# Feed-forward inputs without the norm: differences made from them, gate and up scaled afterwards, pairs from the third block on

## The chip, the cores and the metric

One Trainium2 chip; the kernel runs on one of its cores. A core has TensorE (matmuls, into PSUM), VectorE (DVE in the profile), ScalarE (ACT), GpSimd (POOL) and SyncE (SP), which issues most of the DMA transfers. Each engine takes its instructions in a fixed order and waits by semaphores. The metric is the device time of one execution in microseconds; lower is better.

## The reference

Two layers; each is a half-step feed-forward, a mixer (attention and a state-space part) and a second half-step feed-forward, on 512 positions of 1024 channels, float32.

```
h = rms_norm(x, gain)                    # x * rs(position) * gain(channel)
gate, up = split(h @ w_up)               # 2 x 2816 columns
x = x + 0.5 * ((silu(gate) * up) @ w_down)
```

`rs` is one number per position, so (x * gain) @ w, multiplied by rs afterwards, is h @ w.

## The kernel before, in words

Activations lie with channels on partitions, as eight tiles of 128x512 (`KB` = 8). A float32 product is made of three matmuls (`mm3`, L284 to L286): each operand is split into a rounded part "hi" and a rest "lo", and hi*hi, lo*hi and hi*lo are summed. A weight *unit* is 128x1024: SyncE loads it (`wraw`), ScalarE makes `whi` (L251), VectorE makes `wlo` (L253). `whi` and `wlo` have three buffers, and `convert` is set going two units ahead.

`h` holds the eight (hi, lo) tiles that the matmuls stream. When x is finished, `norm_split` writes them as x * gain, without rs, since rs needs the sum of squares over all channels (`norm_square`, `norm_end`: a matmul with ones, then the root). So a stage starts on unnormalised `h`. Once rs is there, `scale_blocks` (L334) makes normalised tiles `tt`, and at the next "up" `project` swaps: `swapped` (L325, L326) splits `tt` into new tiles, which later units use.

**The feed-forward** (`ffn`) takes 22 blocks of 128 hidden channels in three slices (8, 8, 6); after each slice "down" products add to x. A plain block is two units, gate and up, each 24 matmuls of 512 columns (8 channel tiles x 3). Blocks from `pairs_from` on are taken two at a time by `pair_of_blocks` with seven products of half size in place of eight: inputs and weights are cut into quarters (lower and upper channels; first and second half of the positions; gate and up), and the products, in the order "11", "12", "s2", "s1", "s3", "s4", "22", take quarters or their sums and differences. Each is 24 matmuls of 256 columns. Two use the accumulator `chain` again, so what it holds is copied out by ScalarE between products (`g1`, `g2`, L578, L583). The differences of inputs are made once in a feed-forward by `combine` (L346 to L357; results `th` and `tt`), from normalised tiles, after the swap.

Sums of weights come in two ways. s1 and s3 are made by DMA: SyncE loads a stored block, and GpSimd issues a second transfer that adds another to it (L225). s2 and s4 are added by VectorE (`add`, L236). In a pair g1 and g2 go through `activate` (L565 Silu on ScalarE, L570 product with up on VectorE, then a split).

**What sets the order.** TensorE, VectorE, ScalarE and GpSimd run in the order in which the program writes their instructions. `spawn` adds a generator to a list, and `tick` advances all of them once; a tick comes after each k of a plain product and after every second k in a pair, and `yield n` rests for n ticks. SyncE's issues are ordered by the scheduler.

Of the kernel before, what the change touches and what calls it, by code (L numbers as in the profile page):

```python
# [16 lines left out]
P = 128  # L17
# [70 lines left out]
def pairs_from(layer, f):  # L88

    return 6 if (layer, f) == (0, 1) else 4  # L90
# [49 lines left out]
class Builder:  # L140
# [6 lines left out]
    SPARE = 2  # L147

    def __init__(self, ctx, tc, xT, wflat, par, taps, out):
# [62 lines left out]
    def fetch(self, i):  # L212
# [8 lines left out]
        for key in self.early.get(i, ()):  # L221
            base = key[:-1]
            raw = self.sums[key] = self.t(self.sx, [P, KB * P], key[-1], bufs=2)
            self.nc.sync.dma_start(raw, self.stored(base + ("s1",)))
            self.nc.gpsimd.dma_start(raw, self.stored(base + ("22" if key[-1] == "s1" else "11",)), accum_op=ALU.add)  # L225
# [75 lines left out]
    def project(self, *key, swap=False, aside=False):  # L301
# [5 lines left out]
        if swap and not normed and self.scaled_blocks >= KB // 2:  # L307
# [6 lines left out]
            if self.th is not None:  # L314
                self.spawn(self.combine())
# [23 lines left out]
    def combine(self):  # L339
# [3 lines left out]
        a, b = slice(0, half), slice(half, SEQ)  # L343
        for k in range(KB // 2):
            u, v = self.tt[k], self.tt[k + KB // 2]
            nc.vector.tensor_tensor(u[:, a], u[:, a], u[:, b], op=ALU.subtract)  # L346
# [4 lines left out]
            for i in (k, k + KB // 2):  # L351
                yield 1
                hi = self.th[i]
                nc.scalar.copy(hi, self.tt[i])
                yield 2
                lo = self.t(self.tp, [P, SEQ], "tt", F32R)
                nc.vector.tensor_tensor(lo, self.tt[i], hi.bitcast(F32), op=ALU.subtract)  # L357
                self.diff[i] = (hi, lo)
# [159 lines left out]
    def gate(self, pg, g, normed):  # L518
        nc = self.nc
        if normed:  # L520
            self.tables(False)
            nc.scalar.activation(g, pg, AF.Silu)
        else:
            yield from self.scaled(g, pg)
            yield 3
            self.tables(False)
            nc.scalar.activation(g, g, AF.Silu)
            yield 1
            nc.gpsimd.tensor_tensor(g, g, self.rs, op=ALU.mult)
        self.gated[g.name] = True  # L530
        yield 1
# [9 lines left out]
    def pair_of_blocks(self, base, fp, two):  # L541
# [4 lines left out]
        assert self.normed and self.combined == n  # L546
# [16 lines left out]
        def activate(g, c, cols):  # L563

            nc.scalar.activation(g, g, AF.Silu)  # L565
            yield 1
            while not c:
                yield 1
# [5 lines left out]

        up1, up2 = [], []
# [745 lines left out]
```

## Time and profile before

| | |
|---|---|
| median of 3 runs | 2631.35 us (2630.26 to 2632.52) |
| the profiled execution's own time | 2631.69 us |
| its span, first to last instruction | 2630.0 us |
| TensorE granted clock, mean | 0.997 |
| busy: PE / DVE / ACT / POOL | 99% / 64% / 49% / 15% of the span |
| pairs of blocks | 35 (70 accumulating DMAs of GpSimd) |

Times in rows are microseconds from the span's start. A row of the timeline is: start, length, engine, line, operation, output<-inputs, shapes, count, and in brackets how long the engine was idle before it and what ended that. Successive instructions overlap a little, so their spacing is read from their starts.

### The profile page before, as it was taken

Reading aid. Unit: us, or ns where it says so; the run is one execution under the profiler, and the core shown is the slowest. Engines: PE = TensorE matmul, PEld = TensorE weight load, DVE = VectorE, ACT = ScalarE, POOL = GpSimd, SP = SyncE. Lnnn points to the kernel's source line nnn. Section 1 sums busy time; section 2 is a strip of 40 time slices with the busy share of each in tenths; the row PEclk is TensorE's granted clock in tenths of the full one; section 3 lists DMA queues with packets and bytes.
Section 4 is the critical chain, followed back from the end, with each engine's and each line's share of the span. In section 5 each row is a group of like instructions: output and inputs, shape, how many; then the busy total and the mean of one; then the engine's idle time right before and its main releaser. Section 6 shows DMA issues by size and latency. Waiting matters only on the chain.

```text
span 2630.0 us, 37423 instructions
## 1 busy us (share of the span) xinstructions
PE 2601.0 (99%) x14784; PEld 2282.8 (87%) x14784; DVE 1680.4 (64%) x2322; ACT 1277.5 (49%) x2069; POOL 385.5 (15%) x542
## 2 busy tenths in 40 slices
PE   9999999999999999999999999999999999999998
PEld 6899988888888889899988989888888888899996
DVE  8565675665666468575785746766666754775655
ACT  5343546655554245353553535566555643443444
POOL 2000011133232011000110000112332410200001
PEclk9999999999999999999999999999999999999999
DMA  6555342333333446474354644423333344464632
GB/s 187 143 148 149 105 137 75 97 112 105 109 96 119 142 136 163 120 191 112 124 143 135 169 129 114 128 75 110 102 116 105 97 136 122 134 170 131 175 110 74
DMA packets 101551, 331.59 MB, mean 126 GB/s; under 512 B 11856, under 2 KB 13136, under 8 KB 101376
## 3 DMA queue, kind: packets, MB, share of 16 engines
q1 hardware_dynamic: 91008, 292.43, 35.5%
q0 software_dynamic: 10080, 36.70, 8.1%
q8 instruction: 116, 1.90, 0.3%
q14 instruction: 59, 0.48, 0.1%
q10 hardware_dynamic: 288, 0.07, 0.0%
HBM read 316.48 MB, written 12.68 MB: 125 GB/s over the span
## 4 chain that ended last, share of the span: by engine, by line
PE 86%; DVE 9%; ACT 2%; issue 1%; DMA 1%; POOL 0%; SPq 0%; DVEq 0%; ACTq 0%
PE mm L284 24%; PE mm L286 24%; PE mm L285 24%; PE pa L285 3%; PE pa L286 3%; DVE wlo L253 3%; PE pa L284 3%; PE pa L975 1%; PE pt L738 1%; DVE tt L334 1%; PE pa L812 1%; PE pa L977 1%; DVE hlo L468 1%; PE pt L960 1%; PE pt L958 1%
## 5 line engine op out<-in xcount | busy, mean ns | idle before, releaser
L251 ACT CAST whi<-wraw 128x1024 fp32r<-128x1024 f32 (+2 forms) x437 | 436.7, 999 | 532.6 <-PE mm L286 507.7
L253 DVE TENSOR_TENSOR wlo<-wraw,whi 128x1024 fp32r<-128x1024 f32 (+2 forms) x437 | 541.7, 1240 | 187.8 <-ACT whi L251 185.9
L284 PE MATMUL mm<-hhi,whi 128*128 128x512 f32 (+1 forms) x1728 | 650.3, 376 | 0.0
L286 PE MATMUL mm<-hlo,whi 128*128 128x512 f32 (+1 forms) x1728 | 631.4, 365 | 1.9 <-DVE hlo L326 1.8
L285 PE MATMUL mm<-hhi,wlo 128*128 128x512 f32 (+1 forms) x1728 | 629.3, 364 | 0.7 <-DVE wlo L253 0.6
L286 PEld LDWEIGHTS mm<-hlo,whi 128*128 128x128 f32 x1728 | 326.3, 189 | 57.6 <-DVE hlo L326 3.7
L285 PEld LDWEIGHTS mm<-hhi,wlo 128*128 128x128 f32 x1728 | 327.2, 189 | 47.1 <-DVE wlo L253 1.5
L284 PEld LDWEIGHTS mm<-hhi,whi 128*128 128x128 f32 x1728 | 326.9, 189 | 44.8 <-issue 1.0
L284 PE MATMUL mm<-act,whi 128*128 128x512 f32 x704 | 274.0, 389 | 0.0
L285 PE MATMUL mm<-act,wlo 128*128 128x512 f32 x704 | 274.0, 389 | 0.0
L286 PE MATMUL mm<-act,whi 128*128 128x512 f32 x704 | 273.9, 389 | 0.0
L285 PE MATMUL mm<-th,wlo 128*128 128x256 f32 x840 | 238.0, 283 | 1.7 <-DVE wlo L253 1.7
L286 PE MATMUL mm<-tt,whi 128*128 128x256 f32 x840 | 237.7, 283 | 0.0
L284 PE MATMUL mm<-th,whi 128*128 128x256 f32 x840 | 237.7, 283 | 0.0
L253 DVE TENSOR_TENSOR wlo<-s,whi 128x1024 fp32r<-128x1024 f32 x140 | 171.2, 1224 | 69.2 <-ACT whi L251 68.0
L598 DVE SCALAR_TENSOR_TENSOR x<-mm,x 128x512 f32<-128x512 f32 x96 | 66.1, 688 | 209.0 <-PE mm L286 209.0
L225 POOL DMA_DIRECT2D s<-in_wflat_dram x70 | 60.9, 938 | 915.9 <-DMA s<-in_wflat_dram 417.4
L251 ACT CAST whi<-s 128x1024 fp32r<-128x1024 f32 x140 | 146.4, 1046 | 39.4 <-PE mm L286 39.3
L285 PEld LDWEIGHTS mm<-th,wlo 128*128 128x128 f32 x840 | 161.2, 192 | 2.3 <-DVE wlo L253 2.3
L284 PEld LDWEIGHTS mm<-th,whi 128*128 128x128 f32 x840 | 161.3, 192 | 0.0
L286 PEld LDWEIGHTS mm<-tt,whi 128*128 128x128 f32 x840 | 161.3, 192 | 0.0
L876 DVE SCALAR_TENSOR_TENSOR cv<-mm,conv,cv 128x511 f32<-128x511 f32 (+2 forms) x192 | 142.4, 743 | 24.2 <-ACT cv L873 22.3
(264 smaller groups left out, 4653.4 us busy)
## 6 DMA issues: line engine op xcount, KB each, us to landing
wraw<-in_wflat_dram SPq DMA_DIRECT2D x357, 512.0 KB, 3.7
s<-in_wflat_dram SPq DMA_DIRECT2D x70, 512.0 KB, 5.4
s<-in_wflat_dram POOLq DMA_DIRECT2D x70, 512.0 KB, 7.6
wraw<-in_wflat_dram SPq DMA_DIRECT2D x64, 384.0 KB, 3.0
cumb<-cum_d SPq DMA_DIRECT2D x16, 768.0 KB, 4.2
xd<-x SPq DMA_DIRECT2D x16, 256.0 KB, 4.2
wraw<-in_wflat_dram SPq DMA_DIRECT2D x16, 256.0 KB, 3.2
x<-xd SPq DMA_DIRECT2D x16, 256.0 KB, 5.0
```

Source lines behind the costliest of these rows:

```text
L225: self.nc.gpsimd.dma_start(raw, self.stored(base + ("22" if key[-1] == "s1" else "11",)), accum_op=ALU.add)
L251: nc.scalar.copy(hi[:, :n], raw[:, :n])
L253: nc.vector.tensor_tensor(lo[:, :n], raw[:, :n], hi[:, :n].bitcast(F32), op=ALU.subtract)
L284: mm(ps, a[0], b[0], start=start, stop=False, **kw)
L285: mm(ps, a[1], b[0], start=False, stop=False, **kw)
L286: mm(ps, a[0], b[1], start=False, stop=stop, **kw)
L334: self.nc.vector.scalar_tensor_tensor(self.tt[k], self.x[k], gain[:, k:k + 1], self.rs, op0=ALU.mult, op1=ALU.mult)
L468: nc.vector.scalar_tensor_tensor(lo, x, gain[:, m:m + 1], hi.bitcast(F32), op0=ALU.mult, op1=ALU.subtract)
L598: self.nc.vector.scalar_tensor_tensor(x, pd, 0.5, x, op0=ALU.mult, op1=ALU.add)
L738: self.nc.tensor.transpose(pt[:, cs], src[:, cs], self.ident)
L812: nc.tensor.matmul(pz[:, (i - j) * P:n], lhs, part, start=False, stop=(i == j and part is sps[i][1]), skip_group_check=True)
L876: nc.vector.scalar_tensor_tensor(u[:, i:], ps[:, :SEQ - i], tap[KCONV - 1 - i], u[:, i:], op0=ALU.mult, op1=ALU.add)
```

## The change

- `pairs_from` goes from 4 to 2, and from 6 to 4 in the first feed-forward: one more pair in each of the four.
- In a feed-forward `h` stays x * gain. There is no `scale_blocks`, no swap and no second set of tiles.
- `combine` starts as soon as x is finished (in the first feed-forward 10 ticks after the opening) and makes the differences from x * gain itself, with two ScalarE activations added for each two tiles.
- A plain gate is multiplied by rs on VectorE ahead of Silu and on GpSimd behind it, which scales the product with up as well; before, this was so only for blocks ahead of the swap.
- In a pair, g1 is multiplied by rs on GpSimd ahead of Silu and again behind it; g2 is on VectorE, and the up that goes with it (c) on GpSimd (`normed_up`).
- GpSimd's accumulating transfer for s1 and s3 is issued 9 ticks behind the load (`onto`) instead of at once, and not ahead of the feed-forward's own fifth unit (`first`).
- `norm_end` waits 6 ticks instead of 4 ahead of its matmul.

```diff
 def pairs_from(layer, f):
-    return 6 if (layer, f) == (0, 1) else 4
+    return 4 if (layer, f) == (0, 1) else 2
...
+            if key[2:] == ("gate", 0):
+                first = i + 4
             if "pair" in key and key[-1] in ("s1", "s3"):
-                self.early.setdefault(i - (5 if key[-1] == "s1" else 4), []).append(key)
+                self.early.setdefault(max(first, i - (5 if key[-1] == "s1" else 4)), []).append(key)
...
         for key in self.early.get(i, ()):
-            base = key[:-1]
-            raw = self.sums[key] = self.t(self.sx, [P, KB * P], key[-1], bufs=2)
-            self.nc.sync.dma_start(raw, self.stored(base + ("s1",)))
-            self.nc.gpsimd.dma_start(raw, self.stored(base + ("22" if key[-1] == "s1" else "11",)), accum_op=ALU.add)
+            raw = self.t(self.sx, [P, KB * P], key[-1], bufs=2)
+            self.nc.sync.dma_start(raw, self.stored(key[:-1] + ("s1",)))
+            self.spawn(self.onto(key, raw), 9)
+
+    def onto(self, key, raw):
+        src = self.stored(key[:-1] + ("22" if key[-1] == "s1" else "11",))
+        self.nc.gpsimd.dma_start(raw, src, accum_op=ALU.add)
+        self.sums[key] = raw
+        yield 1
...
-    def combine(self):
+    def combine(self, gain):
...
+        while len(self.h) < KB:
+            yield 1
         for k in range(KB // 2):
-            u, v = self.tt[k], self.tt[k + KB // 2]
-            nc.vector.tensor_tensor(u[:, a], u[:, a], u[:, b], op=ALU.subtract)
+            m = k + KB // 2
+            u, v, x = self.tt[k], self.tt[m], self.x[k]
+            nc.scalar.activation(u[:, b], x[:, b], AF.Copy, scale=gain[:, k:k + 1])
+            nc.scalar.activation(v, self.x[m], AF.Copy, scale=gain[:, m:m + 1])
+            yield 1
+            nc.vector.scalar_tensor_tensor(u[:, a], x[:, a], gain[:, k:k + 1], u[:, b], op0=ALU.mult, op1=ALU.subtract)
             nc.vector.tensor_tensor(u[:, b], v[:, b], u[:, b], op=ALU.subtract)
...
-    def gate(self, pg, g, normed):
+    def gate(self, pg, g):
         nc = self.nc
-        if normed:
-            self.tables(False)
-            nc.scalar.activation(g, pg, AF.Silu)
-        else:
-            yield from self.scaled(g, pg)
-            yield 3
-            self.tables(False)
-            nc.scalar.activation(g, g, AF.Silu)
-            yield 1
-            nc.gpsimd.tensor_tensor(g, g, self.rs, op=ALU.mult)
+        yield from self.scaled(g, pg)
+        yield 3
+        self.tables(False)
+        nc.scalar.activation(g, g, AF.Silu)
+        yield 1
+        nc.gpsimd.tensor_tensor(g, g, self.rs, op=ALU.mult)
...
         def activate(g, c, cols):
+            while self.rs is None:
+                yield 1
+            norm(nc.gpsimd if c is up1 else nc.vector, g, cols)
+            yield 2 if c is up1 else 1
+            self.tables(False)
             nc.scalar.activation(g, g, AF.Silu)
             yield 1
+            if c is up1:
+                norm(nc.gpsimd, g, cols)
+                yield 1
             while not c:
                 yield 1
...
+        def normed_up(c):
+            while self.rs is None:
+                yield 1
+            norm(nc.gpsimd, c, b)
+            up2.append(c)
+
+        def norm(eng, r, cols):
+            r = r.rearrange("p (j t) -> p j t", j=2)
+            eng.tensor_tensor(r, r, self.rs[:, cols].unsqueeze(1).to_broadcast([P, 2, half]), op=ALU.mult)
...
-            yield from self.norm_end(3 if gain is None else 4)
+            yield from self.norm_end(3 if gain is None else 6)
...
-                        pg, normed = self.project(layer, f, "gate", j)
-                        self.spawn(self.gate(pg, g, normed))
-                        pu, _ = self.project(layer, f, "up", j, swap=True)
+                        pg = self.product(self.h, layer, f, "gate", j)
+                        self.spawn(self.gate(pg, g))
+                        pu = self.product(self.h, layer, f, "up", j)
```

How the order moves is seen in three places. First GpSimd, in the second slice of layer 1's first feed-forward (g is the first gate of a pair, c its second up; of two neighbouring `s` the first is s1, the second s3, always those of a pair still to come). Before:

```order
L225 DMA s_2251_13345<-in_wflat_dram 128x1024
L225 DMA s_2258_13412<-in_wflat_dram 128x1024
L225 DMA s_2281_13580<-in_wflat_dram 128x1024
L225 DMA s_2288_13647<-in_wflat_dram 128x1024
L225 DMA s_2311_13815<-in_wflat_dram 128x1024
L225 DMA s_2318_13882<-in_wflat_dram 128x1024
```

And now:

```order
L600 TENSOR_TENSOR g_13587<-g_13587,rs_12487 128x512 x2
L230 DMA s_2227_13619<-in_wflat_dram 128x1024
L230 DMA s_2234_13687<-in_wflat_dram 128x1024
L600 TENSOR_TENSOR c_13718<-c_13718,rs_12487 128x512
L600 TENSOR_TENSOR g_13822<-g_13822,rs_12487 128x512 x2
L230 DMA s_2257_13858<-in_wflat_dram 128x1024
L230 DMA s_2264_13926<-in_wflat_dram 128x1024
L600 TENSOR_TENSOR c_13957<-c_13957,rs_12487 128x512
```

GpSimd's queue held DMA issues alone; now three multiplies of each pair stand between the issues, two of them on the first gate ahead of the issues for the next pair.

Second VectorE in the same slice, from the end of one pair's s4 product to the next pair's second low part. Before:

```order
L591 TENSOR_TENSOR g_13546<-g_13546,pa_13544 128x512
L236 TENSOR_TENSOR s_2299_13750<-s_2281_13580,wraw_13645 128x1024
L570 SCALAR_TENSOR_TENSOR a_13758<-c_13678,g_13546 128x512
L253 TENSOR_TENSOR wlo_13748<-wraw_13680,whi_13747 128x1024
L374 TENSOR_TENSOR act_13541<-a_13758,act_13540 128x2x256
L570 SCALAR_TENSOR_TENSOR a_13788<-mm_13542,g_13545 128x512
L374 TENSOR_TENSOR act_13541<-a_13788,act_13540 128x2x256
L253 TENSOR_TENSOR wlo_13791<-s_2299_13750,whi_13790 128x1024
```

And now:

```order
L619 TENSOR_TENSOR g_13823<-g_13823,pa_13821 128x512
L600 TENSOR_TENSOR g_13823<-g_13823,rs_12487 128x512
L243 TENSOR_TENSOR s_2275_14031<-s_2257_13858,wraw_13924 128x1024
L587 SCALAR_TENSOR_TENSOR a_14046<-c_13957,g_13823 128x512
L260 TENSOR_TENSOR wlo_14029<-wraw_13959,whi_14028 128x1024
L587 SCALAR_TENSOR_TENSOR a_14069<-mm_13819,g_13822 128x512
L387 TENSOR_TENSOR act_13818<-a_14046,act_13817 128x2x256
L387 TENSOR_TENSOR act_13818<-a_14069,act_13817 128x2x256
L260 TENSOR_TENSOR wlo_14073<-s_2275_14031,whi_14072 128x1024
```

The multiply of the second gate (L600) came in ahead of s2's sum (L243), and both splits (L387) stand behind both products (L587). The sum reads the s1 (s_2257) that GpSimd issued in this same pair.

Third VectorE at the start of layer 0's second feed-forward, now, the last operations ahead of the first low part of an s2 (wlo_9223; wlo_9171 is that of "12"):

```order
L358 TENSOR_TENSOR tt_8996<-tt_8997,tt_8996 128x256
L526 TENSOR_TENSOR g_9113<-mm_9114,rs_9088 128x512
L243 TENSOR_TENSOR s_1622_9173<-s_1593_9004,wraw_9002 128x1024
L360 SCALAR_TENSOR_TENSOR tt_8997<-tt_8996,tt_8997 128x256
L361 SCALAR_TENSOR_TENSOR tt_8997<-tt_8997 128x256
L260 TENSOR_TENSOR wlo_9171<-wraw_9055,whi_9170 128x1024
L369 TENSOR_TENSOR tt_9193<-tt_8996,th_8985 128x512
L369 TENSOR_TENSOR tt_9199<-tt_8997,th_8989 128x512
L547 TENSOR_TENSOR a_9220<-mm_9163,g_9113 128x512
L387 TENSOR_TENSOR act_8999<-a_9220,act_8998 128x512
L260 TENSOR_TENSOR wlo_9223<-s_1622_9173,whi_9222 128x1024
```

Before, the rows between the last difference and the first s2 were plain weights and ups; now the last differences (L358 to L369), the second gate and up (L526, L547, L387) and the weights of the first pair (L243, L260) alternate.

More of the change, by code (lines that the diff above doesn't have):

```diff
@@ L146 @@
     ROOM = 3
-    SPARE = 2
     def __init__(self, ctx, tc, xT, wflat, par, taps, out):
@@ L350, in combine @@
             nc.vector.scalar_tensor_tensor(v[:, a], v[:, b], -1.0, v[:, a], op0=ALU.mult, op1=ALU.subtract)
-            for i in (k, k + KB // 2):
-                yield 1
+            yield 1
+            for i in (k, m):
                 hi = self.th[i]
                 nc.scalar.copy(hi, self.tt[i])
-                yield 2
+                yield 1
+            for i in (k, m):
                 lo = self.t(self.tp, [P, SEQ], "tt", F32R)
-                nc.vector.tensor_tensor(lo, self.tt[i], hi.bitcast(F32), op=ALU.subtract)
-                self.diff[i] = (hi, lo)
+                nc.vector.tensor_tensor(lo, self.tt[i], self.th[i].bitcast(F32), op=ALU.subtract)
+                self.diff[i] = (self.th[i], lo)
+                yield 1
             self.combined = k + 1
@@ L581, in pair_of_blocks @@
         self.spawn(activate(g1, up1, a))
+        assert self.combined == n
         product(chain, "s2", diff[n:], b, False)
@@ L622, in ffn @@
                 tc.tile_pool(name=f"ffn{layer}{f}", bufs=3, reuse_waits="tile") as fp, \
-                tc.tile_pool(name=f"hx{layer}{f}", bufs=self.SPARE, reuse_waits="tile") as hx, \
                 tc.tile_pool(name=f"sx{layer}{f}", bufs=2, reuse_waits="tile") as self.sx, \
                 tc.tile_pool(name=f"tt{layer}{f}", bufs=KB + 2, reuse_waits="tile") as tp:
-            self.hx = [self.pair(hx, ("xhi", "xlo")) for _ in range(self.SPARE)]
             self.gated = {}
@@ L632, in ffn @@
             self.tp, self.diff = tp, [None] * KB
-            self.open_norm(tiles, gain)
+            self.tt, self.combined = tiles, 0
+            if self.pos:
+                self.spawn(self.combine(gain))
             for s, (j0, j1) in enumerate(SLICES):
@@ L646, in ffn @@
                     if self.pos == 0:
-                        (pg, pu), normed = self.opening(gain), False
-                        self.spawn(self.gate(pg, g, normed))
-                    else:
-                        pg, normed = self.project(layer, f, "gate", j)
-                        self.spawn(self.gate(pg, g, normed))
-                        pu, _ = self.project(layer, f, "up", j, swap=True)
+                        pg, pu = self.opening(gain)
+                        self.spawn(self.gate(pg, g))
+                        self.spawn(self.combine(gain), 10)
+                    else:
+                        pg = self.product(self.h, layer, f, "gate", j)
+                        self.spawn(self.gate(pg, g))
+                        pu = self.product(self.h, layer, f, "up", j)
                     self.spawn(self.up(pu, g, fp, act[-2 + j % 2]))
@@ L1077, in mixer @@
         self.open_norm(self.x, gain)
-        self.hx, self.th = [], None
+        self.hx = []
         first = []
```

9 lines of the change are left out of this document (4 added, 5 removed).

## The prediction

> **What bounds the kernel now.** I read the shares of the page first, then the chain of waits.
>
> ```profile
> PE 2601.0 (99%) x14784; PEld 2282.8 (87%) x14784; DVE 1680.4 (64%) x2322; ACT 1277.5 (49%) x2069; POOL 385.5 (15%) x542
> PE 86%; DVE 9%; ACT 2%; issue 1%; DMA 1%; POOL 0%; SPq 0%; DVEq 0%; ACTq 0%
> ```
>
> TensorE is never without work for long: the end is set by how many matmuls there are, how closely they follow each other, and by the few places where one waits. VectorE's 64% is a mean over stages, so the stages that the change touches were read next, as windows (columns: length, then busy time of PE, PEld, DVE, ACT, POOL, clock, DMA share, GB/s).
>
> ```profile
> 1465.05:1485.21 20.16, 20.16 (x170) 20.16 (x169) 15.23 (x17) 10.98 (x15) 1.73 (x2) 1.00 0.76 197
> 974.75:1018.50 43.75, 43.19 (x214) 36.57 (x212) 42.49 (x64) 23.39 (x35) 9.20 (x5) 1.00 0.53 142
> ```
>
> The first row is one steady pair: TensorE full, VectorE 15.23 of 20.16 us, GpSimd only two DMA issues. The second is the start of layer 0's second feed-forward, from the norm to the first difference of weights: VectorE busy for 42.49 of 43.75 us. VectorE is a second bound there.
>
> **The change, part by part.** The sum goes against the profiled execution's 2631.69 us (span 2630.0); the median of the runs shown is 2631.35, 0.3 below.
>
> *Four more pairs.* The rows are the first matmuls of two units that follow each other, with 24 matmuls between (start, length).
>
> ```profile
> 58.73 0.39 PE L284 MATMUL mm<-xhi,whi 128*128 128x512 f32 x1
> 64.17 0.39 PE L284 MATMUL mm<-xhi,whi 128*128 128x512 f32 x1
> 86.24 0.28 PE L284 MATMUL mm<-th,whi 128*128 128x256 f32 x1
> 89.12 0.28 PE L284 MATMUL pa<-th,whi 128*128 128x256 f32 x1
> ```
>
> A plain unit takes 64.17 - 58.73 = 5.44 us, a seventh of a pair 2.88. Four units are 21.76, seven sevenths 20.16: 1.6 us less for each pair, and one more pair in each of four feed-forwards: **-6.4 us**. Matmuls of half width follow at 0.12 us, more than half of 0.227, so an eighth fewer products give 7%.
>
> *The waits that go.*
>
> ```profile
> 43.12 0.50 PE L284 MATMUL mm<-xhi,whi 128*128 128x512 f32 x1 [1.70 <-ACT xhi L325]
> 48.12 0.50 PE L286 MATMUL mm<-hlo,whi 128*128 128x512 f32 x1 [1.75 <-DVE hlo L326]
> 368.46 0.70 PE L494 MATMUL pt<-acc,ones 128*128 128x512 f32 x1 [1.24 <-DVE acc L486]
> 1321.15 1.12 PE L494 MATMUL pt<-acc,ones 128*128 128x512 f32 x2 [1.23 <-DVE acc L486]
> 1669.18 0.70 PE L494 MATMUL pt<-acc,ones 128*128 128x512 f32 x1 [1.24 <-DVE acc L486]
> ```
>
> The last three are the norm's sum, issued before its input is there. Two ticks later is two blocks of three matmuls, 6 x 0.227 = 1.36 us, more than the wait; the norm's result is not later for it, since the input sets it: **-3.7 us**. The first two are the swap to normalised inputs in the first feed-forward, which is removed; matmuls behind them are slow for some 2 us more (0.79 and 0.63 for 0.39).
>
> ```profile
> 49.38 0.79 PE L286 MATMUL mm<-hlo,whi 128*128 128x512 f32 x1
> 24.88 3.07 DVE L486 TENSOR_TENSOR acc<-acc,tt 128x512 f32<-128x512 f32 x4
> ```
>
> But VectorE gets the combining there instead. From the end of the squares' sum, 24.88 + 3.07 = 27.9 us, to the low part of the first s2 it has, in the new order, 16 operations of half width at 0.44, 8 splits and 12 gates, ups and their splits at 0.60, 7 of width 1024 at 1.13 and 4 of the norm at 0.70, by the rows shown here: 29.7 us, to 57.6. The product is due two blocks' end later: TensorE is free at 43.12 - 1.70 = 41.4, two units and two sevenths more make 58.0. That fits only without a gap, and the ups in that queue wait for GpSimd. I expect most of the 5.5 us to return as other waits: **-1 us**, with bounds of -5.5 (nothing returns) and +2.
>
> *The other three feed-forward starts.* The first difference product comes two blocks, four units, 21.76 us earlier. What VectorE no longer does before it: eight multiplies by the norm, eight low parts, four weight parts, two ups and two splits.
>
> ```profile
> 987.28 0.74 DVE L334 SCALAR_TENSOR_TENSOR tt<-x,par,rs 128x512 f32<-128x512 f32 x1
> 992.69 1.88 DVE L326 TENSOR_TENSOR hlo<-tt,hhi 128x512 fp32r<-128x512 f32 x3
> 991.55 1.21 DVE L253 TENSOR_TENSOR wlo<-wraw,whi 128x1024 fp32r<-128x1024 f32 x1
> 1018.52 0.39 PE L285 MATMUL mm<-th,wlo 128*128 128x256 f32 x1 [0.58 <-DVE wlo L253]
> 974.75 0.69 DVE L500 TENSOR_SCALAR sq<-pt 128x512 f32<-128x512 f32 x1 [2.91 <-ACT rs L498]
> ```
>
> Following one another they overlap a little (0.60 of 0.68, 1.13 of 1.21): 8 x 0.67 + 8 x 0.60 + 4 x 1.13 + 4 x 0.60 = 17.1 us. So 21.8 - 17.1 = 4.7 us are missing. The combining no longer waits for the norm and fills the 2.91 us of idle time; against that the ups now wait for two GpSimd multiplies with VectorE's queue behind them, some 1.7 us. With the 0.58 of today the wait becomes 0.58 + 4.7 - 2.9 + 1.7 = 4.1 us, 3.5 more: **three times, +10.5 us**. Bounds: +1.8 each (no waits on GpSimd) and +5.5 (slow matmuls behind two long waits, the 2 us of the first feed-forward).
>
> *The steady pairs.* Each gets a multiply on VectorE and three on GpSimd. GpSimd's price for VectorE shows where the two meet:
>
> ```profile
> 959.03 1.34 POOL L486 TENSOR_TENSOR acc<-acc,sq 128x512 f32<-128x512 f32 x1 [4.11 <-ACT sq L479]
> 959.13 2.31 DVE L253 TENSOR_TENSOR wlo<-wraw,whi 128x1024 fp32r<-128x1024 f32 x1
> 991.17 4.88 POOL L529 TENSOR_TENSOR g<-g,rs 128x512 f32<-128x512 f32 x1 [8.69 <-ACT g L527]
> 994.50 0.41 DVE L346 TENSOR_TENSOR tt<-tt 128x256 f32<-128x256 f32 x1
> 994.94 1.40 DVE L347 TENSOR_TENSOR tt<-tt,tt 128x256 f32<-128x256 f32 x1
> ```
>
> A GpSimd multiply that starts first holds VectorE's next two-input operation for 1.1 us (2.31 for 1.21). One that comes while VectorE runs such operations back to back waits until these leave a gap: 4.88 us, and only then L347 is held. In the pair, the rows of VectorE, ScalarE and GpSimd are:
>
> ```profile
> 1471.01 0.69 DVE L580 TENSOR_TENSOR g<-g,mm 128x512 f32<-128x512 f32 x1
> 1471.62 1.22 DVE L236 TENSOR_TENSOR s<-s,wraw 128x1024 f32<-128x1024 f32 x1
> 1473.34 1.22 DVE L253 TENSOR_TENSOR wlo<-s,whi 128x1024 fp32r<-128x1024 f32 x1 [0.50 <-ACT whi L251]
> 1471.74 0.63 ACT L565 ACTIVATE g<-g 128x512 f32<-128x512 f32 x1 [2.06 <-DVE g L580]
> 1467.17 0.62 ACT L369 CAST act<-a 128x512 fp32r<-128x512 f32 x1 [0.77 <-DVE a L570]
> 1473.89 0.59 ACT L583 COPY g<-mm 128x512 f32<-128x512 f32 x1 [0.59 <-PE mm L286]
> 1475.01 0.86 POOL L225 DMA_DIRECT2D s<-in_wflat_dram  x1 [11.15 <-DVE wlo L253]
> s<-in_wflat_dram POOLq DMA_DIRECT2D x70, 512.0 KB, 7.6
> 1483.14 1.22 DVE L236 TENSOR_TENSOR s<-s,wraw 128x1024 f32<-128x1024 f32 x1
> 1484.27 0.69 DVE L570 SCALAR_TENSOR_TENSOR a<-c,g 128x512 f32<-128x512 f32 x1
> 1487.98 0.69 DVE L374 TENSOR_TENSOR act<-a,act 128x512 fp32r<-128x512 f32 x1 [0.69 <-ACT act L369]
> 1488.59 2.50 DVE L253 TENSOR_TENSOR wlo<-s,whi 128x1024 fp32r<-128x1024 f32 x2
> ```
>
> Today GpSimd has only DMA issues there and runs a whole pair ahead. In the new order both issues for the next pair's sums stand behind the two multiplies of this pair's first gate. So a loop closes from pair to pair, each step by its row: low part of s1 1.13, gate sum 0.60, s4's sum 1.13, low part of s3 1.22 (GpSimd waits: the two follow without a gap, since ScalarE has s3 ready before its Silu in the new order), multiply 1.34, Silu 0.63, multiply 1.34, accumulating DMA 7.6 to landing, s2's sum 1.13, product 0.60, low part 1.13, product 0.60, cast 0.62, split 0.60, low part of s2 1.22: 20.9 us, and about 0.2 for hand-overs. The pair takes 20.16: 0.9 us late on each turn. Silu is late with it, and behind Silu stands the copy that must leave the accumulator before s3's product. The first turn of a slice starts without arrears, so I take 0.8. Three, four and three pairs in the slices of a feed-forward are 2 + 3 + 2 turns; four feed-forwards, less one pair: 27. **+21.6 us**. Bounds: 0 (GpSimd gets in after s4's sum: 1.2 less, the loop closes in time) and 33 (landing in 8.0 us: 0.4 more a turn).
>
> The rest costs nothing on the path: weights converted for the added pairs (three more each), and the third GpSimd multiply, which runs while VectorE waits for TensorE's s4; without that cover it is 1.1 us a pair. The last pair of a slice has 5.44 us of down products before its result is due.
>
> Sum: -6.4 - 3.7 - 1 + 10.5 + 21.6 = +21.0; 2631.7 + 21.0 = **2652.7 us**, slower by 0.8%.
>
> **Rivals.** *GpSimd gets its turn* (no change). If its multiply goes in right behind s4's sum, the loop takes 19.9 us and no turn is late: 2652.7 - 21.6 = 2631.1. For and against it:
>
> ```profile
> 35.00 3.83 POOL L529 TENSOR_TENSOR g<-g,rs 128x512 f32<-128x512 f32 x2 [33.37 <-ACT g L527]
> 35.90 4.80 DVE L334 SCALAR_TENSOR_TENSOR tt<-x,par,rs 128x512 f32<-128x512 f32 x4
> 48.21 5.55 POOL L529 TENSOR_TENSOR g<-g,rs 128x512 f32<-128x512 f32 x1 [9.38 <-ACT g L527]
> ```
>
> At 35 us two multiplies went in between operations of L334, which have a scalar pointer (4.80 for four, where 2.7 is usual). At 48 us, and at 991 as shown, one stood behind back-to-back operations, nearly all without a pointer, and those of the pair are of that kind. By the Trainium skill, page SBUF — State Buffer, section Who interferes with whom, the one that issues first takes the shared ports and the other blocks for that instruction alone; by that rule GpSimd would go in here, and the 4.88 us do not agree with it.
>
> *Everything is covered* (faster). The combining at the starts finds its gaps, the loop closes, and the first feed-forward keeps its 5.5 us: 2631.7 - 6.4 - 3.7 - 5.5 = 2616. For it: VectorE's 15.23 us leave 4.9 in a pair, and combining starts before the norm. Against it: 42.49 of 43.75 busy leaves no room for 4.7 us.
>
> *VectorE becomes the bound* (slower still). With 0.6 for its own multiply and 3 x 1.1 held, a pair's 15.23 become 19.1 of 20.16; if transfers land in 8.0 us and the starts cost 5.5 each: 2631.7 - 11.1 + 33 + 16.5 = 2670. It decides from the point where s2's low part ends over 1.2 us later than now.
>
> **How the numbers follow.** Forecast 0.50, GpSimd's turn 0.18, all covered 0.22, VectorE the bound 0.10. A measurement of this kernel tells 0.2%, 5 us, from no change: faster 0.24, same 0.16, slower 0.60 (a little of the second case falls on the fast side). The forecast's own range is 2640 to 2664; both signs weigh, so the range given is 2617 to 2668.
>
> **What would show it.** Right: in steady pairs a wait of 0.4 to 1 us of TensorE before the first s3 or s2 product, ended by ScalarE's copy or VectorE's low part; GpSimd's first gate multiply 2 us or more long; its issue for s1 at 12 to 13.5 us into the pair, not 10; waits of 2 to 5 us at the first pair of three feed-forwards; none before the norm's sum. Wrong: TensorE at 20.16 us for each pair of a slice, which makes the loop a story; multiplies of 1.34 us behind s4's sum, which is the first rival; first pairs that wait under 1 us, which means that I overcounted VectorE's work at the starts.

## The result, and the profile after

| | before | after |
|---|---|---|
| median | 2631.7 us (22 runs, 2630.3 to 2634.3) | 2635.9 us (22 runs, 2633.1 to 2638.0) |
| span of the profiled execution | 2630.0 us | 2634.7 us |
| granted clock, mean | 0.997 | 0.996 |
| pairs of blocks | 35 | 39 |

After / before is 1.0014 (95% interval 1.0008 to 1.0021): slower by 4.2 us, less than the 0.2% that the prediction called no change. It is far from the forecast's 2652.7 and below the forecast's own range (2640 to 2664); it lies inside the range given (2617 to 2668).

The page of the changed kernel: engines, then the chain of waits, one group of instructions and the accumulating transfers.

```profile
PE 2598.5 (99%) x15072; PEld 2296.1 (87%) x15072; DVE 1765.3 (67%) x2330; ACT 1298.4 (49%) x2093; POOL 571.0 (22%) x668
PE 87%; DVE 7%; DMA 2%; ACT 2%; issue 1%; POOL 1%; SPq 0%; DVEq 0%; ACTq 0%; POOLq 0%
L292 PE MATMUL mm<-hhi,wlo 128*128 128x512 f32 (+1 forms) x1840 | 652.9, 355 | 11.6 <-DVE wlo L260 11.6
...
s<-in_wflat_dram POOLq DMA_DIRECT2D x78, 512.0 KB, 8.9
```

TensorE is busy for 2.5 us less than before (four pairs more), the span is 4.7 us longer: it waits more. 11.6 us of its idle time stand in one group, the products that need the low part of a weight (`wlo`) next.

Two stretches as windows (columns as in the prediction): a steady pair, and the start of layer 0's second feed-forward.

```profile
1447.47:1467.62 20.15, 20.15 (x169) 20.15 (x168) 14.79 (x14) 9.95 (x12) 6.69 (x5) 1.00 0.62 145
962.80:1007.40 44.60, 41.21 (x242) 36.02 (x241) 38.51 (x52) 26.61 (x39) 10.84 (x10) 1.00 0.43 109
```

The pair takes what it took before, with TensorE full, although GpSimd went from 1.73 to 6.69 us in it. The start does not. TensorE's larger waits there, and in the other starts, from the timeline:

```profile
47.53 0.50 PE L292 MATMUL mm<-hhi,wlo 128*128 128x512 f32 x1 [1.50 <-DVE wlo L260]
54.80 0.39 PE L292 MATMUL mm<-hhi,wlo 128*128 128x256 f32 x1 [1.65 <-DVE wlo L260]
59.95 0.58 PE L292 MATMUL mm<-hhi,wlo 128*128 128x256 f32 x1 [2.03 <-DVE wlo L260]
991.68 0.39 PE L292 MATMUL mm<-hhi,wlo 128*128 128x256 f32 x1 [1.38 <-DVE wlo L260]
995.72 0.38 PE L291 MATMUL mm<-th,whi 128*128 128x256 f32 x1 [1.02 <-ACT g L605]
997.10 0.39 PE L292 MATMUL mm<-th,wlo 128*128 128x256 f32 x1 [0.99 <-DVE wlo L260]
1343.81 0.58 PE L292 MATMUL mm<-hhi,wlo 128*128 128x256 f32 x1 [3.27 <-DVE wlo L260]
1349.22 0.39 PE L292 MATMUL mm<-th,wlo 128*128 128x256 f32 x1 [0.99 <-DVE wlo L260]
2296.32 0.39 PE L292 MATMUL mm<-hhi,wlo 128*128 128x256 f32 x1 [1.10 <-DVE wlo L260]
366.87 1.13 PE L507 MATMUL pt<-acc,ones 128*128 128x512 f32 x2
```

The last row is the norm's sum: no wait in front of it any more.

For sums over many rows I use TensorE's *excess*: the spacing of successive matmuls beyond 0.227 us (512 columns) or 0.120 (256), added up in stretches of 10 us and counted where a stretch has over 0.3. It takes in the slow matmuls behind a wait. At the four starts:

| kernel | (0,1) | (0,2) | (1,1) | (1,2) | sum | median |
|---|---|---|---|---|---|---|
| before | 6.6 | 0.9 | 0.8 | 0.9 | 9.2 | 2631.7 |
| after | 7.5 | 5.3 | 6.1 | 5.4 | 24.3 | 2635.9 |

(layer, feed-forward). The starts lose 15.1 us more than before. The norm's sums, with the matmuls behind them, lose 4.5 less (7.0 before, 2.5 after), and the four pairs are worth 6.4: 15.1 - 4.5 - 6.4 = +4.2, which is the difference of the medians.

Of the 24.3 us, 16.6 are waits (those of 0.05 us and more) and some 7.6 are matmuls that follow too slowly; before, 5.3 of 9.2 were waits. Many of the slow matmuls run at half the granted clock. Two neighbouring stretches of 3.4 us at the start of layer 1's second feed-forward (columns as above):

```profile
2302.50:2305.90 3.40, 3.40 (x18) 3.40 (x18) 3.40 (x4) 0.18 (x1) 2.19 (x1) 0.50 0.54 167
2305.90:2309.30 3.40, 3.40 (x30) 3.40 (x30) 2.09 (x2) 2.07 (x4) 2.88 (x3) 1.00 0.86 189
```

At a clock of 0.50 TensorE had 18 matmuls, at 1.00 it had 30, and it counts as busy in both. The changed kernel's profiled execution has three such stretches at its starts (from 59.9, 1343.3 and 2302.5 us), with 4.4 of the 7.6 us in them; the one before has one (from 48.6).

### The profile page after: what moved, and what is told of

It is laid out like the page before. It is cut to its first block, busy times and chain, and to the rows that moved or that the text cites. A ratio compares the mean times of both kernels' runs of the same rounds, so it can differ in the third digit from the quotient of the medians.

```text
span 2634.7 us, 38180 instructions
## 1 busy us (share of the span) xinstructions
PE 2598.5 (99%) x15072; PEld 2296.1 (87%) x15072; DVE 1765.3 (67%) x2330; ACT 1298.4 (49%) x2093; POOL 571.0 (22%) x668
## 4 chain that ended last, share of the span: by engine, by line
PE 87%; DVE 7%; DMA 2%; ACT 2%; issue 1%; POOL 1%; SPq 0%; DVEq 0%; ACTq 0%; POOLq 0%
PE mm L291 24%; PE mm L292 24%; PE mm L293 24%; PE pa L292 3%; PE pa L293 3%; PE pa L291 3%; DVE wlo L260 2%; PE pa L1004 1%; PE pt L767 1%; DMA s<-in_wflat_dram 1%; PE pa L841 1%; DVE tt L369 1%; PE pa L1006 1%; PE pt L989 1%; PE pt L987 1%
## 5 line engine op out<-in xcount | busy, mean ns | idle before, releaser
L260 DVE TENSOR_TENSOR wlo<-wraw,whi 128x1024 fp32r<-128x1024 f32 (+2 forms) x433 | 571.6, 1320 | 159.9 <-ACT whi L258 158.3
L292 PE MATMUL mm<-hhi,wlo 128*128 128x512 f32 (+1 forms) x1840 | 652.9, 355 | 11.6 <-DVE wlo L260 11.6
L292 PEld LDWEIGHTS mm<-hhi,wlo 128*128 128x128 f32 x1840 | 350.1, 190 | 56.4 <-DVE wlo L260 14.0
L293 PEld LDWEIGHTS mm<-hlo,whi 128*128 128x128 f32 x1840 | 349.2, 190 | 50.2 <-DVE hlo L481 0.3
L291 PEld LDWEIGHTS mm<-hhi,whi 128*128 128x128 f32 x1840 | 349.7, 190 | 41.4 <-issue 1.0
L600 POOL TENSOR_TENSOR g<-g,rs 128x512 f32<-128x512 f32 x78 | 144.3, 1850 | 753.3 <-DVE g L607 724.3
L260 DVE TENSOR_TENSOR wlo<-s,whi 128x1024 fp32r<-128x1024 f32 x156 | 230.7, 1495 | 60.6 <-ACT whi L258 59.6
L292 PE MATMUL mm<-th,wlo 128*128 128x256 f32 x936 | 266.2, 284 | 3.0 <-DVE wlo L260 3.0
L291 PE MATMUL mm<-th,whi 128*128 128x256 f32 x936 | 265.8, 284 | 2.0 <-ACT g L605 2.0
L293 PE MATMUL mm<-tt,whi 128*128 128x256 f32 x936 | 265.5, 284 | 0.0
```

The lines of the kernel that those rows point to most:

```text
L260: nc.vector.tensor_tensor(lo[:, :n], raw[:, :n], hi[:, :n].bitcast(F32), op=ALU.subtract)
L291: mm(ps, a[0], b[0], start=start, stop=False, **kw)
L292: mm(ps, a[1], b[0], start=False, stop=False, **kw)
L293: mm(ps, a[0], b[1], start=False, stop=stop, **kw)
L600: eng.tensor_tensor(r, r, self.rs[:, cols].unsqueeze(1).to_broadcast([P, 2, half]), op=ALU.mult)
```

## The experiments

Times are medians; the kernel before stayed between 2631.6 and 2632.3 in all of them, and each ratio is to it.

**The pairs back to where they started.** In the changed kernel:

```diff
 def pairs_from(layer, f):
-    return 4 if (layer, f) == (0, 1) else 2
+    return 6 if (layer, f) == (0, 1) else 4
```

> The changed kernel with the pairs starting where they started before (fourth block, sixth in the first feed-forward), everything else as changed. Theory (the loss sits in the starts, because VectorE's queue of combining, plain blocks and first weights ends too late for a pair two blocks earlier): four pairs fewer cost 4 x 1.6 = +6.4, and the starts' waits, 7.4 + 5.4 + 6.1 + 5.4 = 24.3 us of TensorE in the changed kernel's trace, fall to about 1 each: 2635.8 + 6.4 - 20 = 2622 us, below both kernels. Rival (the loss is the multiplies by the norm that each of 35 remaining pairs keeps): the starts give back little, 2639 to 2642. In the trace: theory, under 1.5 us of waits at each start; rival, the waits there stay at 4 us or appear in the pairs.

Measured: **2622.2 us**, ratio 0.9959 (0.9946 to 0.9973), as the theory had it. The excess at the starts is 3.7 us, all in the first feed-forward (the theory had about 1 at each). Of this kernel's page, engines and the same group as above:

```profile
PE 2597.4 (99%) x14784; PEld 2282.7 (87%) x14784; DVE 1733.3 (66%) x2302; ACT 1281.7 (49%) x2069; POOL 555.1 (21%) x656
L292 PE MATMUL mm<-hhi,wlo 128*128 128x512 f32 (+1 forms) x1904 | 682.5, 358 | 3.5 <-DVE wlo L260 3.5
```

So the earlier start is what loses: 24.3 - 3.7 = 20.6 us of excess for 6.4 us of pairs, 14.2 on balance; 13.7 measured. Without the swap, with 35 pairs that each scale their products, the kernel is 9.5 us faster than before; the later norm's sum is part of that (next run).

**The norm's sum later, alone.** In the kernel before:

```diff
-            yield from self.norm_end(3 if gain is None else 4)
+            yield from self.norm_end(3 if gain is None else 6)
```

> The kernel before with one edit: the norm's sum is issued 6 ticks, not 4, after its input's last tile. Theory: its three waits (1.24, 1.23, 1.24 us) vanish and nothing is later for it, since the input sets the norm's end: -3.7, 2631.7 - 3.7 = 2628.0. Rival: in the kernel before, the multiplies by the norm and the swap follow the norm's end, and the sum now runs up to 1.4 us later: the wait comes back at the swap or at the first pair, 2631 to 2633.

Measured: 2629.7 us, ratio 0.9992 (0.9983 to 1.0001), 2.6 us below the kernel before, though the interval just reaches 1. In the trace the excess around the three sums falls by 4.3 us, and each of the three starts behind them gets 0.4 more (0.9, 0.8 and 0.9 become 1.3 each): net -3.1. The profiled execution took 2631.97 us all the same: at the first feed-forward's start, ahead of every sum that the edit moves, it lost 2.3 us more than the kernel before, with a granted clock of 0.50 from 52 to 54 us where the other had 0.99. Both expectations hold in part: most of the term is real, and over a quarter comes back at the starts. That it is the swap's wait for the norm that brings it back is not shown.

**The loop from pair to pair.** In `activate` of the changed kernel, once and then three times:

```diff
                 norm(nc.gpsimd, g, cols)
+                nc.gpsimd.tensor_tensor(spare, g, self.rs, op=ALU.mult)
```

> The changed kernel with one GpSimd multiply more in each pair (g by the norm into a spare tile that nothing reads), behind the second multiply of g1 and ahead of the two accumulating transfers of the next pair. Theory (the loop from pair to pair is there as reckoned and only the place where GpSimd gets in was wrong, so its slack is small: in the trace the transfer for s1 lands at 1466.24 and VectorE's sum for s2 starts at 1466.45): the transfers land about 1.3 us later, and each of 27 turns becomes 0.8 to 1.2 us longer than 20.16: +21 to +32, 2657 to 2668. Rival (no such loop: the transfer is wanted much later, or its landing is not set by GpSimd's issue): pairs stay at 20.16 and the time within 3 us of 2636.

> The changed kernel with three spare GpSimd multiplies in each pair instead of the one of the run before. There the transfer for s1 was issued 2.25 us later and landed at the same place in the pair, 5.5 us after its issue instead of 7.7, 0.13 us ahead of VectorE's sum. Theory (the loop is there, but the time to landing is mostly waiting behind another load, and 5.5 is its floor): the issue now comes 2.6 to 4.4 us later again and lands as much later; the low part of s2 had 1.0 us to spare, so each turn from pair to pair is 1.6 to 3.4 us longer: 27 turns, +43 to +92, 2679 to 2728. Rival (nothing waits for the transfer): pairs stay at 20.16, 2636 to 2638.

Measured: 2636.3 us (1.0013, 1.0004 to 1.0023) with one, **2776.4 us** (1.0549, 1.0533 to 1.0565) with three. The first expectation failed: next to nothing was lost. In the trace three turns are late, by 3.1 us together (2.2 of them in the first feed-forward, where VectorE's sum at 80.61 waits 3.10 us for the transfer); the others stay at 20.15 or 20.16. GpSimd in the second pair of a slice, first of the changed kernel, then with one multiply more:

```profile
1454.19 2.20 POOL L600 TENSOR_TENSOR g<-g,rs 128x512 f32<-128x512 f32 x1 [52.06 <-DVE g L607]
1457.14 1.50 POOL L600 TENSOR_TENSOR g<-g,rs 128x512 f32<-128x512 f32 x1 [0.74 <-ACT g L579]
1458.59 1.76 POOL L230 DMA_DIRECT2D s<-in_wflat_dram  x2
```

```profile
1456.46 2.20 POOL L602 TENSOR_TENSOR g<-g,rs 128x512 f32<-128x512 f32 x1 [52.05 <-DVE g L609]
1459.40 1.50 POOL L602 TENSOR_TENSOR g<-g,rs 128x512 f32<-128x512 f32 x1 [0.74 <-ACT g L579]
1460.98 2.18 POOL L584 TENSOR_TENSOR spare<-g,rs 128x512 f32<-128x512 f32 x1
1463.10 1.76 POOL L230 DMA_DIRECT2D s<-in_wflat_dram  x2
```

From the first multiply to the issue it is 4.40 us in the one and 6.64 in the other: 2.24 later in the pair. The first of the two transfers, from issue to landing, in the changed kernel and then in the other:

```profile
s<-in_wflat_dram POOLq DMA_DIRECT2D x1, 512.0 KB, 7.7
```

```profile
s<-in_wflat_dram POOLq DMA_DIRECT2D x1, 512.0 KB, 5.5
```

Issued 2.2 us later, it landed 2.2 us sooner after its issue, at the same place. The shortest of all these transfers took 5.3 us in the changed kernel and 5.1 here; in the changed kernel SyncE's load for s3 was in flight (issued at 1457.50, landed at 1462.65), in the other it had only 1.2 us to go. From issue to landing the DMA engines' mean share was 0.97 in the one and 0.78 in the other. So I read a part of the 7.6 us of my loop as waiting behind other transfers, which a later issue does not add to. The Trainium skill, page DMA: Bandwidth & Descriptors, section Issuing engines are not separate DMA queues, says that transfers run on the same 16 DMA engines and interleave whoever issues them; these two rows agree.

With three multiplies more the floor is reached, and the loop shows. GpSimd, VectorE and then TensorE in that kernel:

```profile
1562.85 5.77 POOL L585 TENSOR_TENSOR spare<-g,rs 128x512 f32<-128x512 f32 x3
...
1574.77 1.23 DVE L243 TENSOR_TENSOR s<-s,wraw 128x1024 f32<-128x1024 f32 x1 [2.56 <-DMA s<-in_wflat_dram]
1575.91 0.68 DVE L590 SCALAR_TENSOR_TENSOR a<-c,g 128x512 f32<-128x512 f32 x1
1576.51 1.22 DVE L260 TENSOR_TENSOR wlo<-wraw,whi 128x1024 fp32r<-128x1024 f32 x1
...
1577.78 0.39 PE L292 MATMUL mm<-hhi,wlo 128*128 128x256 f32 x1 [2.54 <-DVE wlo L260]
```

VectorE stands at s2's sum for the transfer, and what TensorE then misses is not s2 but the weights of "12", queued behind the sum. Late turns take 24.5 to 27 us instead of 20.16, so 4.3 to 6.8 more, where I gave 1.6 to 3.4. TensorE's waits in them are 2.4 to 4.2 us: the issue came 3.6 us later than with one multiply, as expected (three took 5.8 to 7.0 us, since they held up, or were held up by, low parts), but this transfer took 6.2 us to landing, not 5.5. The rest is slow matmuls (mean granted clock 0.93 in the turn from 1574.96). The first turn of the second and third slices stays at 20.15.

The changed kernel shows the same loop once, without any multiply more, from the first pair of layer 0's second feed-forward to its second (VectorE, TensorE):

```profile
1012.27 1.23 DVE L243 TENSOR_TENSOR s<-s,wraw 128x1024 f32<-128x1024 f32 x1 [1.90 <-DMA s<-in_wflat_dram]
1015.29 0.38 PE L292 MATMUL mm<-hhi,wlo 128*128 128x256 f32 x1 [0.66 <-DVE wlo L260]
```

That turn takes 21.31 us. Two others are late, by 0.21 and 0.55 us, and in both VectorE's sum waits about 1 us for the transfer: 1.9 us together.

**What the starts wait for.** Five edits of the changed kernel; all but the last leave a part of the computation out, as their expectations say. In `combine`:

```diff
-                nc.vector.tensor_tensor(lo, self.tt[i], self.th[i].bitcast(F32), op=ALU.subtract)
+                nc.scalar.copy(lo, self.tt[i])
```

> The changed kernel where the low parts of the input differences are not computed by VectorE: ScalarE copies the tile in their place (the rest that the rounding leaves is left out of these products, so the values are not the reference's). VectorE has 8 operations of 0.60 = 4.8 us less ahead of the first pair, ScalarE 8 of 0.5 to 0.6 more. Theory (VectorE's queue sets the starts): the waits at each start fall by 3.5 to 4.8 us, together 24.3 to 7 or 9: 2635.8 - 15 to -17 = 2619 to 2621. Rival (the waits come from hand-overs to ScalarE and GpSimd: the ups behind GpSimd's multiply, the copy of g1 late on ScalarE): they fall by under 1.5 us each or grow, 2631 to 2640.

In `gate`:

```diff
-        nc.gpsimd.tensor_tensor(g, g, self.rs, op=ALU.mult)
```

> The changed kernel without GpSimd's multiply of a plain gate behind Silu (the norm's second factor is left out of the plain blocks, so the values are not the reference's); VectorE's work is the same. Theory of hand-overs: the start's queues stand where VectorE's product with up waits for Silu and then GpSimd, and ScalarE's split behind it waits for VectorE; without the multiply each start loses 2 to 3 us of waits and holds (two multiplies of 1.3 to 1.6, one hold of 0.9 and one of 1.1 us on VectorE), 2635.8 - 6 to -10 = 2626 to 2630. Rival (the amount in VectorE's queue alone): nothing comes free, under 0.5 us each, 2634 to 2636.

Both:

> Both at once: the low parts of the differences as ScalarE copies, and no second multiply of the plain gates (both leave out part of the computation). Theory of hand-overs and amount together: with the low parts alone the time came down 3.2 us only, since VectorE then stood idle for 1.5 us twice in each start before the product with up; without the multiply that idle time goes as well, and the starts keep under 2 us of waits each: 2635.8 - 14 to -18 = 2618 to 2622. Rival (ScalarE's order is the limit, or weights that are converted too late by the order of the program): the two edits together give no more than the sum of each alone, about 2626 to 2630.

In `combine`, no low parts at all:

```diff
-                lo = self.t(self.tp, [P, SEQ], "tt", F32R)
-                nc.vector.tensor_tensor(lo, self.tt[i], self.th[i].bitcast(F32), op=ALU.subtract)
-                self.diff[i] = (self.th[i], lo)
+                self.diff[i] = (self.th[i], self.th[i])
```

> The changed kernel where the low parts of the input differences are not made at all: the high part is streamed a second time in their place (the low parts are left out, so the values are not the reference's). VectorE loses 8 x 0.60 = 4.8 us in each start, and nothing is added anywhere, unlike the run in which ScalarE made copies instead. Theory (the amount in VectorE's queue counts one to one, and ScalarE's eight copies gave most of it back in that run; up scaled on VectorE costs 2632.1 - 2624.0 = 8.1 us for ten operations of 0.60, which says the same): the starts' 24.3 us of waits fall by 3 to 4.8 us each, 2635.8 - 12 to -19 = 2617 to 2624. Rival (the hand-overs to ScalarE and GpSimd alone set the starts): as with the copies, about 3 us, 2631 to 2634.

In `up`, without GpSimd's multiply in `gate`:

```diff
         a = self.t(fp, [P, SEQ], "a")
-        self.nc.vector.tensor_tensor(a, pu, g, op=ALU.mult)
+        yield from self.scaled(a, pu)
+        while not self.gated.pop(g.name, False):
+            yield 1
+        self.nc.vector.tensor_tensor(a, a, g, op=ALU.mult)
```

> The changed kernel, where a plain block's up is multiplied by the norm on VectorE as soon as it is there (then by the gate), in place of GpSimd's multiply of the gate behind Silu: the same values, one VectorE operation of 0.60 more in each plain block, no GpSimd in its path. Theory of hand-overs: the run that left the multiply out came to 2624.0; two operations more in each of four starts with a full VectorE queue add up to 4 x 1.2, 2624 to 2629. Rival (amount in VectorE's queue decides after all): the operations that are added cost as much as the hand-overs did, 2632 to 2637.

| edit | (0,1) | (0,2) | (1,1) | (1,2) | excess | median | ratio (interval) |
|---|---|---|---|---|---|---|---|
| low parts by ScalarE | 5.4 | 3.8 | 6.7 | 3.8 | 19.7 | 2632.7 | 0.9999 (0.9990 to 1.0008) |
| no gate multiply | 2.6 | 2.0 | 4.1 | 1.8 | 10.5 | 2624.0 | 0.9970 (0.9959 to 0.9981) |
| both | 3.0 | 2.7 | 4.9 | 2.7 | 13.3 | 2626.9 | 0.9981 (0.9972 to 0.9991) |
| no low parts | 3.8 | 2.4 | 4.4 | 1.0 | 11.6 | 2624.4 | 0.9968 (0.9955 to 0.9980) |
| up on VectorE | 4.9 | 4.8 | 6.0 | 3.2 | 18.9 | 2632.1 | 1.0001 (0.9992 to 1.0011) |

Low parts by ScalarE, both edits and up on VectorE came out in their rivals' ranges; no gate multiply came 2 us below its theory's, no low parts 0.4 above its theory's. 4.8 us of VectorE work less in each start bring 3.2 us in all if ScalarE gets copies for it, and 11.5 if nobody does. A multiply of 1.3 to 1.6 us on GpSimd, twice or four times a start, is worth 11.8: more than I had expected. Moved to VectorE as ten operations of 0.60, the same factor gives 8.1 of the 11.8 back. And the edits don't add up: with ScalarE's copies, leaving out the multiply as well ends 2.8 us above leaving out the multiply alone. Neither theory, hand-overs alone or amount alone, holds. I read the start as one chain in which three engines take turns, and any of them can hold it; no run tests that reading by itself. The timeline of layer 1's first feed-forward in the changed kernel, ScalarE and then VectorE, shows one such place:

```profile
1338.33 1.03 ACT L258 CAST whi<-wraw 128x1024 fp32r<-128x1024 f32 x1
...
1337.87 1.29 DVE L369 TENSOR_TENSOR tt<-tt,th 128x512 fp32r<-128x512 f32 x2
1339.08 0.48 DVE L357 SCALAR_TENSOR_TENSOR tt<-x,par,tt 128x256 f32<-128x256 f32 x1
1339.66 0.42 DVE L358 TENSOR_TENSOR tt<-tt,tt 128x256 f32<-128x256 f32 x1
1340.01 0.68 DVE L526 TENSOR_TENSOR g<-mm,rs 128x512 f32<-128x512 f32 x1
1340.61 1.22 DVE L243 TENSOR_TENSOR s<-s,wraw 128x1024 f32<-128x1024 f32 x1
1341.74 0.42 DVE L360 SCALAR_TENSOR_TENSOR tt<-tt,tt 128x256 f32<-128x256 f32 x1
1342.19 0.42 DVE L361 SCALAR_TENSOR_TENSOR tt<-tt 128x256 f32<-128x256 f32 x1
1342.54 1.22 DVE L260 TENSOR_TENSOR wlo<-wraw,whi 128x1024 fp32r<-128x1024 f32 x1
```

The weights' high part is ready at 1339.36; VectorE comes to the low part at 1342.54, TensorE waits 3.27 us for it. In the kernel with the low parts on ScalarE, VectorE has idle time in this start and nothing that it may do in it, since its next operation waits for GpSimd:

```profile
1333.23 0.69 DVE L547 TENSOR_TENSOR a<-mm,g 128x512 f32<-128x512 f32 x1 [1.56 <-POOL g L539]
...
1342.78 0.69 DVE L547 TENSOR_TENSOR a<-mm,g 128x512 f32<-128x512 f32 x1 [1.50 <-POOL g L539]
```

**The order in the queue.** On the kernel with up on VectorE, `convert` makes the low part of the first pair's "12" at once instead of two ticks later.

```diff
-        yield 2
+        if key[-1] != "12" or self.keys[i - 2][2] != "up":
+            yield 2
```

> The kernel with the up scaled on VectorE and the pairs from the third block on, where the low part of the first pair's second weights (12) stands in VectorE's queue ahead of the sum for s2 and two combining operations (1.13 + 2 x 0.45 = 2.0 us) instead of behind them. Theory (what is left at the starts is the order in VectorE's queue: in layer 1's first feed-forward the wait of 2.3 to 3.3 us ends with this low part, whose high part had been ready for over 3 us): 1.5 to 2 us less there, up to 1 in the others, 2 to 4 us below the same kernel in the old order. Rival (the queue is full, and whatever is put first makes the next one late): within 1 us of it.

Measured: 2638.3 us (1.0021, 1.0012 to 1.0031), 6.2 slower than in the old order; the excess at the starts goes from 18.9 to 26.9. Neither expectation has that number. The rival's reason is seen: in layer 1's first feed-forward the wait for "12" shrinks from 2.92 us to 0.98, and one of 2.88 opens at s2, whose product must wait until ScalarE has copied g1 (L605). ScalarE had stood idle for one of the input differences, which VectorE now makes behind the low part and the sum:

```profile
1341.86 0.39 PE L293 MATMUL mm<-hhi,wlo 128*128 128x256 f32 x1 [0.98 <-DVE wlo L261]
1347.76 0.58 PE L292 MATMUL mm<-th,whi 128*128 128x256 f32 x1 [2.88 <-ACT g L605]
1343.83 0.62 ACT L366 CAST th<-tt 128x512 fp32r<-128x512 f32 x1 [3.10 <-DVE tt L362]
```

But the waits at all starts add up to 14.8 us for 13.1 in the old order. Most of the loss, 12.0 for 5.6 us, is slow matmuls: in the profiled execution the granted clock is 0.50 for 6.8 us at three starts and for 3.4 at the fourth, in the old order's for 3.4 us at one. So this run does not show that the new order is the worse one by its waits.

**The second factor behind the down products.**

```diff
-        self.nc.vector.scalar_tensor_tensor(x, pd, 0.5, x, op0=ALU.mult, op1=ALU.add)
+        self.nc.vector.scalar_tensor_tensor(pd, pd, 0.5, rs, op0=ALU.mult, op1=ALU.mult)
+        self.nc.vector.tensor_tensor(x, x, pd, op=ALU.add)
```

with the second multiplies of g and the multiply of c removed.

> The changed kernel with the norm's second factor taken out of the blocks and put behind the down products: no second multiply of a gate, none of c, and x gets 0.5 x down x norm in two VectorE operations instead of one (the same values as the reference). Theory: the starts come down as without the multiply (by the run of that), pairs stay at 20.16, and the end of each feed-forward is 0.7 us later where x is waited for: 2626 to 2633. Rival: the second VectorE operation on x costs at every slice's end, where the products follow, 12 times 0.7: 2634 to 2640.

Measured: 2642.2 us (1.0039, 1.0024 to 1.0054), above both ranges. The excess at the starts comes down from 24.3 to 10.4 us, but at three ends of a feed-forward it rises by 5.5 to 6.9. The last slice's end becomes VectorE's: its rows there repeat every 5.1 us (1316.18 to 1321.30), 4.4 in the changed kernel, where a down unit of six tiles takes TensorE 18 x 0.227 = 4.1. One of these rows, the low part, takes 2.33 us for 1.22 while GpSimd adds a square of the norm beside it, in both kernels.

```profile
1316.18 0.69 DVE L619 SCALAR_TENSOR_TENSOR mm<-mm,rs 128x512 f32<-128x512 f32 x1
1316.90 0.69 DVE L620 TENSOR_TENSOR x<-x,mm 128x512 f32<-128x512 f32 x1
1318.38 0.75 DVE L481 SCALAR_TENSOR_TENSOR hlo<-x,par,hhi 128x512 fp32r<-128x512 f32 x1 [0.79 <-ACT hhi L479]
1319.05 2.33 DVE L260 TENSOR_TENSOR wlo<-wraw,whi 128x1024 fp32r<-128x1024 f32 x1
1321.30 0.69 DVE L619 SCALAR_TENSOR_TENSOR mm<-mm,rs 128x512 f32<-128x512 f32 x1
```

**The best of them.** Up on VectorE, with the pairs where they started before.

> The same edit on the kernel with the pairs starting where they started before, which took 2622.2 and has two waits of 1.5 us left, both in the first feed-forward. Theory of hand-overs: these waits shrink by 1 to 3 us together, the other starts have nothing left to give, 2619 to 2622. Rival (amount): 18 blocks get 0.60 more on VectorE, the waits grow, 2623 to 2626.

Measured: **2621.3 us**, ratio 0.9960 (0.9945 to 0.9975), 0.9 below the kernel without that edit, which the intervals do not tell apart. Its excess at the starts is 2.5 us. Of the kernels that compute everything, these two are the ones clearly below both.

## Why the prediction was wrong

**The steady pairs.** The sum had +21.0; measured were +4.2. The step that failed is the last term, *the steady pairs*, +21.6: in the profiled execution it is worth 1.9 us, since all but three of the 27 turns go without loss (pairs of a slice follow at 20.15 or 20.16 us). It failed at two places of the loop.

- "The two follow without a gap", so that GpSimd waits for both. It waited for one. GpSimd's first gate multiply and the low part of s3 in the changed kernel:

```profile
1474.35 2.21 POOL L600 TENSOR_TENSOR g<-g,rs 128x512 f32<-128x512 f32 x1 [10.23 <-DVE g L607]
```

```profile
1474.18 1.22 DVE L243 TENSOR_TENSOR s<-s,wraw 128x1024 f32<-128x1024 f32 x1
1475.32 2.32 DVE L260 TENSOR_TENSOR wlo<-s,whi 128x1024 fp32r<-128x1024 f32 x1
```

It goes in behind s4's sum and holds the next operation for 1.1 us, in each of the 39 pairs. The prediction named a first gate multiply of 2 us or more as a sign that it was right, and 2.2 came; but the wait in it is for one operation, where the loop has two. That is the first rival's mechanism, in its words and its price (1.2 us less), and the Trainium skill's page SBUF — State Buffer, section Who interferes with whom, which the first rival named, agrees in all 39.

- "Accumulating DMA 7.6 to landing", as a constant. The runs with more multiplies showed that it is not: 2.2 us of later issue cost nothing that the intervals tell (2636.3 us for 2635.9). The loop exists (with three multiplies it costs 5 us a turn), but it had nearly those 2.2 us of slack beside the 1.2. By the prediction's own sum it took both errors to make the term: with GpSimd's place put right the loop takes 19.9 us, with a transfer 2.2 us shorter 18.9, both less than the pair's 20.16.

**The starts**, +10.5 for three and -1 for the first: the mechanism was right and the size too small. Measured are 5.3, 6.1 and 5.4 us where the sum had 4.1, and 7.5 for the first feed-forward where it had 5.6 (6.6 - 1): 15.1 more than before, for 9.5. At the three starts the waits themselves are 3.4, 4.3 and 3.1 us, close to the 4.1 of the sum. Beyond them stand 1.2 us of the late turn at 1012 and nearly 5 of slow matmuls; the sum put these at nothing, and only the bound of +5.5 each allowed for them. In the first feed-forward the waits grew from 3.6 to 5.2 us, where I expected 1 us less in all. Whether the "1.7 us" for ups that wait for GpSimd was the right size is not shown: leaving that multiply out took 13.8 us off the excess, leaving the low parts out took 12.7, and since 13.8 and 12.7 are together more than the 24.3 there was to lose, no single term can be read from either.

**The norm's sum**, -3.7: measured -4.5 in the changed kernel, with the slow matmuls behind the waits. In the kernel before, the same edit gives over a quarter of it back at the starts. My reading is that the swap there still needs the norm early; the change removes the swap.

**Four more pairs**, -6.4: the spans of the runs with and without them agree with it within 0.5 us: 2634.7 - 2620.1 = 14.6 for 20.5 more of excess in the whole program, so 5.9.

**The rivals.** *GpSimd gets its turn* gave 2631.1 and came nearest: its place for GpSimd was right, and what it misses is the starts. *Everything is covered* was wrong at the starts, though its 2616 is what the kernel with late pairs would take if 4 more pairs came without waits (2622.2 - 6.4). *VectorE becomes the bound* did not happen in the pairs (14.79 of 20.15 us busy); it did at the end of a feed-forward, when I gave VectorE an operation more there.

## What to carry to other kernels

A duration from issue to landing is no latency: part of it is other transfers, and a later issue can land at the same time; before it goes into a loop, look for the shortest one in the trace. At a place where several in-order queues hand over to each other, the gain of an edit is not the length of the operation: here a removed multiply was worth more, a moved one less. Try the removal alone before building on it, and split what a start loses into waits and slow matmuls: two orders whose waits differ by 1.6 us differed by 6.2 in time. A change that bundles a cheaper form (no swap, scaling afterwards) with an earlier use of it should be run in halves: here the form, with the later norm's sum, is worth 9.5 us, and the earlier use costs 13.7.

## What was not expected of the hardware

GpSimd's waiting differs by place, and I can't say why. In the kernel before, four multiplies (at 48, 991, 1339 and 2292 us) waited for 3.5 us and more while VectorE ran five or six two-input operations in a row, among them the swap's L326. In the changed kernel none waits for more than one, though the rows of VectorE look alike, also between two splits (L369) at 1344 us. By the rule of the Trainium skill, page SBUF — State Buffer, section Who interferes with whom, as I read it, none should wait for more than the operation that is running; the four rows of the kernel before do not agree with it. Nothing was tried that tells these apart, so it stays open which of the two a new order of VectorE will give.

The granted clock goes by a pattern that I did not expect either. In the traces of all runs here it changes on a grid of 3.41 us, which lies differently in each execution. The half clock began 45 times before the programs' ends, each time behind a cell of the grid in which TensorE was busy for 1.77 us or less; of over 10000 other cells at full clock none had less than 1.60. So the waits ahead of it need not be long: in the changed kernel's cell from 2299.1 us (1.39 us busy) they are 1.03 and 1.00 us. And where the grid lies is chance: at layer 0's second feed-forward waits of 1.02 and 0.99 us fell into two cells, of 2.94 and 1.87 us, and the clock stayed full.
